# A 32-expert mixture stage: which experts are fetched early, the order of its matmuls, and its tables in fp32r

## The chip, the cores and the metric

One Trainium2 chip, one of its cores. The metric is the device time of one execution in microseconds; less is better. The kernel works on one sequence of 512 tokens with 1024 features, all in float32 ("fp32r" is the 32-bit type that TensorE takes in one pass where fp32 takes two; the kernel splits a number into an fp32r part and what is left of it where it needs both).

## The reference

Four layers run one after the other. The first two each have a mixer (three kinds of sequence mixing side by side) and then a mixture of experts. The last two are hybrid layers (two kinds of linear attention, then a layer norm). The change lies in the mixture, which in each of the first two layers computes:

```python
g_sel = top_1(x @ w_group + b_group)            # one of 4 groups for each token
e_local = top_2(expert logits of that group + bias)   # 2 of its 8 experts
weights = p_group * renormalised p_expert       # 2 weights for each token
# for every token and each of its two experts e:
h = silu(x @ w1[e]) * (x @ w3[e])               # 1024 -> 256
out[token] += weight * (h @ w2[e])              # 256 -> 1024
```

So 1024 pairs of a token and an expert are spread over 32 experts, unevenly. An expert's three matrices are 1 MB each, 96 MB for one layer, which don't fit on the core: they are streamed from HBM once for each layer.

## The kernel before

**Slots and groups.** The program is fixed, the routing isn't. `_slots` (L46) therefore lays out 12 groups of 128 slots. Each group is cut into strips of 32, and a position p (0 to 31) owns one, two or three strips of one group: 3 positions with 96 slots (B), 10 with 64 (M), 19 with 32 (S), in the order of `TURNS`. At run time experts are ranked by their token counts, and the expert of rank p takes position p. Tokens that don't fit go through a loop (`more`, L1363), which runs as often as windows of 64 are left over; with these inputs that is zero times, but the test for it is in the program, before group 8 (`CHECK`).

**Early experts.** Routing is done token tile by token tile (4 tiles of 128) beside the last matmuls of the mixer. After two tiles, `router_first` (L1133) takes the three experts with most tokens so far, gives them ranks 0, 1 and 2 for good, and starts to fetch them: 0 and 1 into the pool `wa`, 2 (started after a later chunk, L545) into the pool of width one, `hp`. Positions 0 and 1 are B and 2 is M. The order of the other 29 is known only after the fourth tile. Groups 0 to 3 hold the positions (2, 13, 14), (0, 15), (4, 16, 17), (1, 18).

**Streaming.** Five experts are resident at once: two in `wa`, two in `wp`, one in `hp`. `load` (L1201) gives each new expert the buffer of the resident one whose group is over first. All loads go through SyncE's queue, which is in order: first the new expert's w1 and w3, then the w2 that the expert before it is still owed. Each waits until the matmuls that read the evicted matrix are done. After the first two layers' mixture, the first weights of the next layer go the same way (`stage`), and are split into two fp32r parts by ScalarE and VectorE (`load_first`, pinned in the order of the program).

**The work of a group g** (main loop at the end of `moe_layer`, L1410 on):
- `one_hot`: for the next two groups, a 512 x 256 matrix that says which token sits in which slot (VectorE); once for every two groups.
- `gather`: brings the tokens into slot order, 8 blocks of 8 matmuls (L1237, L1238), an eviction each; once for every two groups, at odd g for g+1 and g+2.
- `up`: 128 matmuls on 32-column strips (L1310), then tanh on ScalarE (L1313) and two VectorE instructions (L1314, L1316).
- `table`: 4 matmuls of fp32, each in two passes (L1292), that give each slot its token and weight; then small VectorE work.
- `turned`: 2 transposes (L1323), evicted by ScalarE (L1325). `down`: 32 matmuls (L1341), evicted as two fp32r parts (L1343, L1344).
- `combine`: adds the group's results to the 512 tokens, 8 steps of 2 matmuls (L1354) and a VectorE add (L1355).

**What sets the order.** The loop is written as up, tables, gather and combine of the group before in turns, turned, down. But a planner reorders each engine's instructions at build time by its own idea of when each is ready; an engine then runs its list in order. Only an instruction passed to `keep_in_program_order` stays behind the one that was written before it on its engine. In the experts' stage before the change no matmul is pinned.

Of the kernel before, what the change touches and what calls it, by code (L numbers as in the profile page):

```python
# [9 lines left out]
F32 = mybir.dt.float32  # L10
# [35 lines left out]
def _slots():  # L46


    turns = TURNS.replace(" ", "")
    kinds = sorted(turns)  # L50
    kinds = kinds[0:2] + ["M"] + kinds[2:turns.count("B")] + kinds[turns.count("B") + 1:]
    size = [dict(B=BIG, M=MID, S=SMALL)[k] for k in kinds]
    free = {k: [p for p in range(len(kinds)) if kinds[p] == k] for k in "BMS"}
    assert len(size) == NE and sum(size) % 128 == 0
# [12 lines left out]
    return [base[p] for p in range(NE)], groups  # L67


BASE, GROUPS = _slots()  # L70
# [14 lines left out]
class Kernel:  # L85
# [42 lines left out]
    def constants(self):  # L128
# [21 lines left out]
        with self.tc.tile_pool(name="ctmp", bufs=1) as tp:  # L150
# [15 lines left out]
            for p in range(NE):  # L166
                b, c = BASE[p]
                nc.gpsimd.memset(self.tab[:, 0, p:p + 1], float(b))
                nc.gpsimd.memset(self.tab[:, 1, p:p + 1], float(c))
# [298 lines left out]
    def mix_layer(self, l, x, xp, xd):  # L468
        nc, a, tc = self.nc, self.a, self.tc
        with ExitStack() as st:  # L470
# [57 lines left out]
            for c, ts in ((0, (0, 1)), (1, (0, 1)), (2, (0, 1)), (3, (0,)), (3, (1,)),  # L528
# [15 lines left out]
                if (c, t) == (1, 3):  # L544
                    W[2] = self.expert_weights(l, third())  # L545
# [587 lines left out]
    def router_first(self, l, rp, wa, R):  # L1133
# [3 lines left out]
        cnt, scr = R["pc"][0], R["scr"]  # L1137
        m8 = rp.tile([128, 8], F32, name="fm8")
        i8 = rp.tile([128, 8], U32, name="fi8")
        V.max(m8, cnt)  # L1140
        V.max_index(i8, m8, cnt)
        fi = rp.tile([128, 3], F32, name="ffi")
        V.tensor_copy(fi, i8[:, 0:3])
        first = rp.tile([1, 3], I32, name="first")
        V.tensor_copy(first, fi[0:1])
        key = R["key"] = rp.tile([128, NE], F32, name="key")
        for i in range(3):
            V.tensor_scalar(scr, self.iota[:, 0:NE], fi[:, i:i + 1], 65536.0 * (3 - i), op0=OP.is_equal, op1=OP.mult)
# [32 lines left out]
    def moe_layer(self, l, x, wa, wp, W, R, hT, nxt=None):  # L1181
        nc, a, tc = self.nc, self.a, self.tc
        V = nc.vector
        with ExitStack() as st:
# [6 lines left out]
            held = {wa: [0, 1], wp: [], None: [2]}  # L1191
# [36 lines left out]
            def gather(oh, n, tag="st"):  # L1228

                m = 4 if tag == "st" else KT  # L1230
                for k in range(KT):
# [3 lines left out]
                    for t in range(NT):  # L1235
                        ts = slice(t * 128, (t + 1) * 128)
                        nc.tensor.matmul(p, hh[:, k, ts], oh[:, t], start=(t == 0), stop=False)  # L1237
# [36 lines left out]
            tv = mp.tile([128, NT, 4], F32, name="tv")  # L1274
            V.tensor_copy(tv[:, :, 0:1], self.tokv)
# [10 lines left out]
            V.tensor_copy(tv[:, :, 2:4], pw.rearrange("p i t -> p t i"))  # L1286

            def table(oh, base, s0, m):

                p = self.mx([m, 4])  # L1290
                for t in range(NT):
                    nc.tensor.matmul(p, oh[:, t, s0:s0 + m].bitcast(F32), tv[:, t], start=(t == 0), stop=(t == NT - 1))  # L1292
                f = mp.tile([m, 4], F32, name="tf", tag="tf", bufs=3)
                V.tensor_copy(f, p)
# [828 lines left out]
```

## Time and profile before

| | us |
|---|---|
| median of 3 runs (1758.17 to 1760.28) | 1758.62 |
| the profiled execution | 1759.24 |
| its span, first to last instruction | 1757.2 |
| experts' stage, layer 0: first gather to the last `down` | 266.4 |
| experts' stage, layer 1 | 265.3 |

The profiled execution is 0.6 us over the median. The profile's page gives busy time by engine (PE is TensorE's matmuls, PEld its weight loads, DVE VectorE, ACT ScalarE, SP SyncE), and in 40 slices the granted TensorE clock (1.00 is full speed) and the share of the transfer engines in use. The views behind it are the stretches of time with busy time of each engine, the waits (who waited for whom), and the instructions in order of time, where a bracket gives the idle time before an instruction and what ended it. A row of the last kind may merge instructions of one line that follow each other; its time then runs from the start of the first to the end of the last, and the next row can start before that end, since matmuls are pipelined.

### The profile page before, as it was taken

The numbers are of one execution on the slowest core, as the hardware profiler recorded it, in microseconds if no ns is written. First come the engines' busy times: TensorE is split into PE (matmuls) and PEld (weight loads), VectorE is DVE, ScalarE is ACT, GpSimd is POOL, SyncE is SP. The second block draws the span as 40 slices with busy tenths as digits, with TensorE's granted clock in tenths as the row PEclk, the third lists the DMA queues.
The fourth block names the chain that finished last, engine by engine and source line by source line (L and its number), as shares of the span: only waits on it lengthen the run. The fifth ranks groups of instructions, "written<-read, shape, count | busy, mean of one in ns | idle before, by whom it ended". The sixth has DMA issues, their size and how long they took to land. (4 is left out here: it accounts for less than half of the span.)

```text
span 1757.2 us, 38728 instructions
## 1 busy us (share of the span) xinstructions
PE 1640.4 (93%) x15762; PEld 1329.8 (76%) x15762; DVE 1069.5 (61%) x2777; ACT 679.7 (39%) x1807; POOL 126.4 (7%) x236
## 2 busy tenths in 40 slices
PE   7999997999999899998799999999999999999998
PEld 7779987665554777998766556487789898778988
DVE  6866755455444586676545545456767565676756
ACT  5656563111111565656311111145443424554340
POOL 1011011000000001102100000000000200000010
PEclk9999998999999999999799999999999999999999
DMA  5112315799897311231679989633311324231132
GB/s 161 44 44 82 112 49 241 286 421 392 315 419 268 119 45 44 82 113 49 258 292 419 374 331 418 259 122 81 88 52 51 122 73 129 74 88 51 51 121 72
DMA packets 132542, 299.22 MB, mean 170 GB/s; under 512 B 34160, under 2 KB 100670, under 8 KB 107784
## 3 DMA queue, kind: packets, MB, share of 16 engines
q1 hardware_dynamic: 129384, 287.46, 44.8%
q10 hardware_dynamic: 1760, 6.30, 0.9%
q0 software_dynamic: 1216, 2.93, 0.7%
q8 instruction: 126, 2.06, 0.5%
q14 instruction: 56, 0.46, 0.1%
HBM read 284.87 MB, written 9.44 MB: 167 GB/s over the span
## 5 line engine op out<-in xcount | busy, mean ns | idle before, releaser
L327 PE MATMUL acc<-w_hi,hT_hi 128*128 128x256 f32 (+2 forms) x1248 | 358.3, 287 | 3.6 <-ACT hT_hi L252 1.6
L328 PE MATMUL acc<-w_lo,hT_hi 128*128 128x256 f32 (+2 forms) x1248 | 356.9, 286 | 1.5 <-DVE w_lo L308 1.4
L329 PE MATMUL acc<-w_hi,hT_lo 128*128 128x256 f32 (+2 forms) x1248 | 353.5, 283 | 3.0 <-issue 1.7
L327 PEld LDWEIGHTS acc<-w_hi,hT_hi 128*128 128x128 f32 x1248 | 237.3, 190 | 8.0 <-ACT hT_hi L252 2.0
L329 PEld LDWEIGHTS acc<-w_hi,hT_lo 128*128 128x128 f32 x1248 | 237.8, 191 | 4.3 <-issue 1.9
L328 PEld LDWEIGHTS acc<-w_lo,hT_hi 128*128 128x128 f32 x1248 | 237.4, 190 | 3.8 <-DVE w_lo L308 2.3
L1310 PE MATMUL acc<-w,xt 128*32 128x256 f32 x3072 | 191.0, 389 | 5.9 <-DVEq L1366 5.9
L1310 PEld LDWEIGHTS acc<-w,xt 128*32 128x32 f32 x3072 | 104.3, 112 | 87.2 <-issue 25.7
L328 PE MATMUL acc<-hT_lo,w_hi 128*128 128x512 f32 x352 | 143.4, 407 | 0.0
L329 PE MATMUL acc<-hT_hi,w_lo 128*128 128x512 f32 x352 | 142.4, 405 | 0.0
L327 PE MATMUL acc<-hT_hi,w_hi 128*128 128x512 f32 x352 | 142.0, 403 | 0.0
L1237 PE MATMUL acc<-oh,hT_hi 128*128 128x256 f32 x384 | 100.4, 297 | 7.1 <-DVE oh L1225 3.4
L1341 PE MATMUL mx<-w,gT 128*32 128x512 f32 x768 | 92.1, 622 | 8.7 <-ACT gT L1325 8.6
L308 DVE TENSOR_TENSOR w_lo<-st,w_hi 128x1024 fp32r<-128x1024 f32 (+2 forms) x71 | 87.4, 1240 | 19.8 <-ACT w_hi L307 19.7
L1313 ACT ACTIVATE th<-acc 128x256 f32<-128x256 f32 x24 | 9.2, 385 | 227.6 <-PE acc L1310 227.6
L1238 PE MATMUL acc<-oh,hT_lo 128*128 128x256 f32 x384 | 96.6, 287 | 0.0
L307 ACT ACTIVATE w_hi<-st 128x1024 fp32r<-128x1024 f32 (+1 forms) x71 | 74.8, 1073 | 49.2 <-PE acc L329 28.6
L1344 DVE SCALAR_TENSOR_TENSOR yb<-mx,ws,yb 128x512 fp32r<-128x512 f32 x48 | 35.9, 748 | 93.3 <-ACT yb L1343 93.3
L1237 PEld LDWEIGHTS acc<-oh,hT_hi 128*128 128x128 f32 x384 | 75.7, 197 | 21.2 <-issue 8.5
L327 PEld LDWEIGHTS acc<-hT_hi,w_hi 128*128 128x128 f32 x352 | 68.1, 193 | 14.4
L1238 PEld LDWEIGHTS acc<-oh,hT_lo 128*128 128x128 f32 x384 | 75.9, 198 | 2.0
L328 PEld LDWEIGHTS acc<-hT_lo,w_hi 128*128 128x128 f32 x352 | 67.1, 191 | 13.6 <-issue 0.3
(607 smaller groups left out, 3195.8 us busy)
## 6 DMA issues: line engine op xcount, KB each, us to landing
w<-in_w_dram SPq DMA_DIRECT2D x192, 1024.0 KB
st<-in_w_in_dram SPq DMA_DIRECT2D x66, 512.0 KB
st<-in_w_out_dram SPq DMA_DIRECT2D x32, 512.0 KB
st<-in_w_in_dram SPq DMA_DIRECT2D x22, 520.0 KB
xd<-x ACTq DMA_DIRECT2D x12, 512.0 KB
x<-xd SPq DMA_DIRECT2D x12, 512.0 KB
x<-in_x_dram SPq DMA_DIRECT2D x8, 512.0 KB
out_dram<-x SPq DMA_DIRECT2D x8, 256.0 KB
```

The source lines that it names most:

```text
L307: q = [nc.scalar.activation(hi[:, sl], w, AF.Copy), nc.vector.tensor_tensor(lo[:, sl], w, hi[:, sl].bitcast(F32), op=OP.subtract)]
L308: nc.vector.tensor_tensor(lo[:, sl], w, hi[:, sl].bitcast(F32), op=OP.subtract)]
L327: self.nc.tensor.matmul(out, lh(k), rh(k), start=(k == ks[0]), stop=False)
L328: self.nc.tensor.matmul(out, lh(k), rl(k), start=False, stop=False)
L329: self.nc.tensor.matmul(out, ll(k), rh(k), start=False, stop=(k == ks[-1]))
L1237: nc.tensor.matmul(p, hh[:, k, ts], oh[:, t], start=(t == 0), stop=False)
L1238: nc.tensor.matmul(p, hl[:, k, ts], oh[:, t], start=False, stop=(t == NT - 1))
L1310: nc.tensor.matmul(ph[c:c + n, i], xt[k][:, s0 + c:s0 + c + n], w[i][:, k], start=(k == 0), stop=(k == KT - 1))
L1313: nc.scalar.activation(th, ph[:, 0], AF.Tanh, scale=0.5)
L1341: nc.tensor.matmul(py[c:c + n], gT[:, k, c:c + n], w[2][:, k, sl], start=(k == 0), stop=(k == 1))
L1344: V.scalar_tensor_tensor(yb[:, 1, sl], py, ws, yb[:, 0, sl].bitcast(F32), op0=OP.mult, op1=OP.subtract)
```

## The change

Three parts.

**Which experts come first.** Position 0 is now M and the B positions are 1 to 3. `router_first` ranks by count (ties by number), and takes the expert of rank 3 after two tiles for position 0, and the two with the fewest tokens for positions 30 and 31. The first group is now made of exactly these three, (0, 30, 31), then (1, 13), (4, 14, 15), (2, 16). Number and size of the early loads stay.

**The order of matmuls.** The first matmul of each block of the experts' stage (gather, up, both transposes, down, combine, table) is pinned; of `up` only the first one for w1, not the first one for w3. The loop is rewritten: after `up`, six steps of the combine of the group before (at odd g in turns with seven blocks of the gather), then `turned`, then the rest, then `down`. At group 7, before the test for left-over windows, the gather goes in turns with the combine of group 7 itself, which stood alone behind the loads of group 8 before. In the last group the next layer's first weights are loaded and split ahead of `up`, not behind `down`.

**Tables.** The four columns of token, slot and weights are kept as an fp32r part and a remainder, 8 columns, so that a table takes 4 one-pass matmuls; a small sum over the two parts replaces the copy.

```diff
 def _slots():
...
-    kinds = kinds[0:2] + ["M"] + kinds[2:turns.count("B")] + kinds[turns.count("B") + 1:]
+    kinds.remove(turns[0])
+    kinds.insert(0, turns[0])
...
+    free["S"] = free["S"][-2:] + free["S"][:-2]
...
+FIRST = (0, NE - 2, NE - 1)
+RANK = 3
...
     def router_first(self, l, rp, wa, R):
...
-        V.max(m8, cnt)
-        V.max_index(i8, m8, cnt)
+        V.scalar_tensor_tensor(key, cnt, float(NE), self.keyc, op0=OP.mult, op1=OP.add)
+        V.tensor_scalar(scr, key, -1.0, None, op0=OP.mult)
+        for i, k in enumerate((key, scr)):
+            V.max(m8[:, i], k)
+            V.max_index(i8[:, i], m8[:, i], k)
...
-        return {i: self.expert_weights(l, e(i), wa) for i in range(2)}, lambda: e(2)
+        return {FIRST[i]: self.expert_weights(l, e(i), wa) for i in range(2)}, lambda: e(2)
...
+                        if t == 0:
+                            tc.keep_in_program_order(q)
...
             tv = mp.tile([128, NT, 4], F32, name="tv")
+            tv2 = mp.tile([128, NT, 8], F32R, name="tv2")
...
+                V.tensor_copy(tv2[:, :, 0:4], tv)
+                V.tensor_tensor(tv2[:, :, 4:8], tv, tv2[:, :, 0:4].bitcast(F32), op=OP.subtract)
...
-                p = self.mx([m, 4])
+                p = self.mx([m, 8])
...
-                V.tensor_copy(f, p)
+                V.reduce_sum(f, p.rearrange("p (i n) -> p n i", i=2), axis=AX.X)
...
             for g in range(n):
                 loads(GROUPS[g])
                 if g == CHECK:
-                    run(combine(*last))
-                    last = None
                     more()
-                ahead = g % 2 and g + 1 < n
+                if g == n - 1:
+                    later()
+                    if nxt:
+                        self.staged = self.stage(nxt[0][0], wp)
+                        self.load_first(*nxt[0])
+                ahead, check = g % 2 and g + 1 < n, g + 1 == CHECK
...
-                sums = combine(*last) if last else None
-                if ahead:
-                    xt_next = []
-                    for step in gather(oh, 256):
-                        xt_next.append(step)
+                sums, rows, xt_next = combine(*last) if last else None, gather(oh, 256) if ahead else None, []
+                for i in range(8 if rows and not check else 6):
+                    if not check:
+                        run(rows, 1 if i < 7 else 0, xt_next)
+                    if i < 6:
                         run(sums, 1)
+                gT = turned(gg, 128)
+                if not check:
+                    run(rows, None, xt_next)
                 run(sums)
-                gT = turned(gg, 128)
                 last = down(gT, segs, 128, *tabs.pop(0))
+                if check:
+                    sums, last = combine(*last), None
+                    for i in range(8):
+                        run(rows, i % 2, xt_next)
+                        run(sums, 1)
+                    run(rows, None, xt_next)
                 if ahead:
                     xt, tabs = xt_next, tables(oh, g + 1)
-                if g == n - 1:
-                    later()
-                    if nxt:
-                        self.staged = self.stage(nxt[0][0], wp)
-                        self.load_first(*nxt[0])
             run(combine(*last, nxt and nxt[1]))
```

## Rows read from the trace of the kernel before

**Rows 1.** The page: busy time of each engine, share of the span, instructions.

```profile
PE 1640.4 (93%) x15762; PEld 1329.8 (76%) x15762; DVE 1069.5 (61%) x2777; ACT 679.7 (39%) x1807; POOL 126.4 (7%) x236
```

**Rows 2.** Stretches: the experts' stages of layers 0 and 1; from PEclk on: clock, transfers.

```profile
304.96:571.40 266.44, 248.23 (x2600) 155.81 (x2600) 130.12 (x311) 37.55 (x76) 0.00 (x0) 0.96 0.87 350
874.19:1139.50 265.31, 247.49 (x2600) 156.12 (x2600) 130.04 (x311) 37.41 (x73) 0.00 (x0) 0.97 0.88 353
```

**Rows 3.** Waits of TensorE, 304.9 to 582: total us, times, longest.

```profile
PE mx L1323 <- DVE gg L1316: 8.5, 7, 1.7
PE mx L270 <- DVE nss L446: 5.6, 1, 5.6
PE mx L1341 <- ACT gT L1325: 4.3, 8, 0.6
```

**Rows 4.** TensorE in order of time, start of the stage: start, us, line, count.

```profile
304.96 0.58 PE L1237 MATMUL acc<-oh,hT_hi 128*128 128x256 f32 x1 [1.33 <-DVE oh L1225]
...
316.17 1.95 PE L1292 MATMUL mx<-tv,oh 128*128 128x4 f32 x16
...
322.47 8.24 PE L1310 MATMUL acc<-w,xt 128*32 128x256 f32 x122
...
333.24 3.64 PE L1341 MATMUL mx<-w,gT 128*32 128x512 f32 x32 [0.47 <-ACT gT L1325]
```

**Rows 5.** TensorE in order of time, the last group.

```profile
556.86 7.10 PE L1310 MATMUL acc<-w,xt 128*32 128x256 f32 x124
565.62 0.41 PE L1323 MATMUL mx<-ident,gg 128*128 128x128 f32 x2 [1.66 <-DVE gg L1316]
566.56 5.34 PE L1341 MATMUL mx<-w,gT 128*32 128x512 f32 x32 [0.53 <-ACT gT L1325]
```

**Rows 6.** TensorE in order of time, one odd group in the middle.

```profile
384.40 0.73 PE L1354 MATMUL acc<-yb,to 128*128 128x512 f32 x2
...
394.67 0.38 PE L1323 MATMUL mx<-ident,gg 128*128 128x128 f32 x2
...
395.58 3.64 PE L1341 MATMUL mx<-w,gT 128*32 128x512 f32 x32
399.15 1.95 PE L1292 MATMUL mx<-tv,oh 128*128 128x4 f32 x16
400.96 0.94 PE L1354 MATMUL acc<-yb,to 128*128 128x512 f32 x3
...
404.99 7.09 PE L1310 MATMUL acc<-w,xt 128*32 128x256 f32 x122
```

**Rows 7.** All engines in order of time, behind the test for left-over windows.

```profile
496.08 8.91 PE L1310 MATMUL acc<-w,xt 128*32 128x256 f32 x132 [2.93 <-DVEq L1366]
```

**Rows 8.** Stretches of layer 0; the last two columns: transfer share, GB/s.

```profile
320.00:327.50 7.50, 6.73 (x78) 3.72 (x82) 2.86 (x9) 0.00 (x0) 0.00 (x0) 0.77 0.02 5
340.00:400.00 60.00, 58.95 (x622) 39.19 (x614) 32.11 (x68) 10.23 (x20) 0.00 (x0) 1.00 1.01 417
...
305.00:555.00 250.00, 233.99 (x2435) 149.12 (x2436) 123.66 (x299) 35.07 (x69) 0.00 (x0) 0.97 0.90 363
```

**Rows 9.** Waits of SyncE's transfer queue, 303 to 560: total, times, longest.

```profile
SPq L1177 <- PE acc L1310: 81.5, 18, 18.5
...
SPq L1177 <- PEq L1366: 5.5, 1, 5.5
```

**Rows 10.** SyncE in order of time, the next layer's first weights.

```profile
552.95 1.18 SPq L287 DMA_DIRECT2D st<-in_w_in_dram  x1
```

**Rows 11.** ScalarE and VectorE in order of time, end of layers 0 and 1's experts.

```profile
572.55 3.29 ACT L311 ACTIVATE w_hi<-st,again 128x256 fp32r<-128x256 f32 x8
...
573.88 3.25 DVE L312 SCALAR_TENSOR_TENSOR w_lo<-st,again,w_hi 128x256 fp32r<-128x256 f32 x8
...
1142.83 2.31 DVE L308 TENSOR_TENSOR w_lo<-st,w_hi 128x2080 fp32r<-128x2080 f32 x1
```

**Rows 12.** VectorE in order of time, `router_first` of layer 0.

```profile
264.80 0.20 DVE L1140 MAX8 fm<-mx 128x8 f32<-128x32 f32 x1 [0.86 <-PE mx L1119]
```

More of the change, by code (lines that the diff above doesn't have):

```diff
@@ L66, in _slots @@
             b, c = b + m, c - m
-    return [base[p] for p in range(NE)], groups
-BASE, GROUPS = _slots()
+    return [base[p][0] for p in range(NE)], size, groups
+BASE, SIZE, GROUPS = _slots()
+FIRST = (0, NE - 2, NE - 1)
+RANK = 3
 ALPHA = (2.0 * 2) ** 0.25
@@ L1188, in moe_layer @@
             rp = R["pool"]
-            held = {wa: [0, 1], wp: [], None: [2]}
+            held = {wa: list(FIRST[0:2]), wp: [], None: [FIRST[2]]}
             ends = {p: g for g, segs in enumerate(GROUPS) for _, _, p in segs}
@@ L1236, in gather @@
                         ts = slice(t * 128, (t + 1) * 128)
-                        nc.tensor.matmul(p, hh[:, k, ts], oh[:, t], start=(t == 0), stop=False)
+                        q = nc.tensor.matmul(p, hh[:, k, ts], oh[:, t], start=(t == 0), stop=False)
+                        if t == 0:
+                            tc.keep_in_program_order(q)
                         nc.tensor.matmul(p, hl[:, k, ts], oh[:, t], start=False, stop=(t == NT - 1))
@@ L1286, in moe_layer @@
             V.tensor_copy(tv[:, :, 2:4], pw.rearrange("p i t -> p t i"))
+            pack()
             def table(oh, base, s0, m):
-                p = self.mx([m, 4])
+                p = self.mx([m, 8])
                 for t in range(NT):
-                    nc.tensor.matmul(p, oh[:, t, s0:s0 + m].bitcast(F32), tv[:, t], start=(t == 0), stop=(t == NT - 1))
+                    o, w = oh[:, t, s0:s0 + m], tv2[:, t]
+                    q = nc.tensor.matmul(p, *((o, w) if m == 128 else (o.bitcast(F32), w.bitcast(F32))), start=(t == 0),
+                                         stop=(t == NT - 1))
+                    if t == 0 and m == 128:
+                        tc.keep_in_program_order(q)
                 f = mp.tile([m, 4], F32, name="tf", tag="tf", bufs=3)
-                V.tensor_copy(f, p)
+                V.reduce_sum(f, p.rearrange("p (i n) -> p n i", i=2), axis=AX.X)
                 c = mp.tile([m, 2], F32, name="tc", tag="tc", bufs=2)
@@ L1309, in up @@
                         for c, n, w in segs:
-                            nc.tensor.matmul(ph[c:c + n, i], xt[k][:, s0 + c:s0 + c + n], w[i][:, k],
-                                             start=(k == 0), stop=(k == KT - 1))
+                            q = nc.tensor.matmul(ph[c:c + n, i], xt[k][:, s0 + c:s0 + c + n], w[i][:, k],
+                                                 start=(k == 0), stop=(k == KT - 1))
+                            if i == k == 0 and m == 128:
+                                tc.keep_in_program_order(q)
                 th = mp.tile([m, DE], F32, name="th", tag="th", bufs=1)
@@ L1322, in turned @@
                 for k in range(2):
[L1323 removed]
+                    q = nc.tensor.transpose(pT[:, k], g[:, k], self.ident[0:m, 0:m])
+                    if m == 128:
+                        tc.keep_in_program_order(q)
                 gT = mp.tile([128, 2, m], F32, name="gT", tag="gT", bufs=1)
@@ L1340, in down @@
                         for c, n, w in segs:
-                            nc.tensor.matmul(py[c:c + n], gT[:, k, c:c + n], w[2][:, k, sl],
-                                             start=(k == 0), stop=(k == 1))
+                            q = nc.tensor.matmul(py[c:c + n], gT[:, k, c:c + n], w[2][:, k, sl],
+                                                 start=(k == 0), stop=(k == 1))
+                            if k == 0 and m == 128:
+                                tc.keep_in_program_order(q)
                     nc.scalar.activation(yb[:, 0, sl], py, AF.Copy, scale=ws)
@@ L1353, in combine @@
                         for i in range(2):
-                            nc.tensor.matmul(p, to[:, t * 128:(t + 1) * 128], yb[:, i, sl], start=(i == 0), stop=(i == 1))
+                            q = nc.tensor.matmul(p, to[:, t * 128:(t + 1) * 128], yb[:, i, sl], start=(i == 0), stop=(i == 1))
+                            if i == 0 and not rows and to.shape[0] == 128:
+                                tc.keep_in_program_order(q)
                         V.tensor_tensor(x[:, t, sl], p, x[:, t, sl], op=OP.add)
```

24 lines of the change are left out of this document (13 added, 11 removed).

## The prediction

> **What bounds the kernel now.** I read the page first: TensorE is busy 93% of the span and no other engine above 61% [rows 1]. The change touches only the experts' stage of two layers, 266.4 and 265.3 us long; there TensorE is busy 248 and 247 us and the transfer engines 0.87 and 0.88 of the time at 350 GB/s [rows 2]. So two things are nearly full in this stage, and both need a count.
>
> TensorE first. The pieces at full clock: an `up` 7.05 us (128 matmuls, 7.09 for 122 with the tail), a `down` 3.57 (395.58 to 399.15), a pair of tables 1.81 (399.15 to 400.96), a combine that stands alone 4.03 (400.96 to 404.99), seven gather blocks in turns with eight combine steps 10.27 (384.40 to 394.67), so about 0.9 a gather block and 0.46 a combine step; a pair of transposes 0.35 [rows 6]. Without waits the stage is 10.7 for the first gather, 5 x 7.3 more of gather, 12 x 7.05 of up, 12 x 3.57 of down, 6 x 1.81 of tables, 11 x 8 x 0.46 of combine, 12 x 0.35 of transposes: 230 us. The stage takes 266, so some 36 us go elsewhere. The waits show the larger part of the causes: the transposes wait 8.5 us in seven groups for the gated product gg, the `down` that follows 4.3 us in eight groups for ScalarE's copy [rows 3], and 2.9 us go at the test for left-over windows [rows 7]. The pattern is in the last group: combine has already run ahead of `up`, nothing is left to do while gg is made, 1.66 and then 0.53 us are idle, and the `down` behind these gaps takes 5.34 instead of 3.6 us [rows 5]. The `up` behind the test takes 8.91 [rows 7], and one at the start 8.24 [rows 4], in a stretch in which the granted clock is 0.77 on the mean, part of it at the lower level [rows 8]. The rest are fragments of `up` and of the gather that the planner put between other blocks.
>
> Transfers second. Where they are never short of work they move 417 GB/s, so 1 MB takes 2.5 us [rows 8]. 29 experts of three loads are 87 loads, 217 us, of the 250 us between 305 and 555; the share of 0.90 says the same [rows 8]. SyncE's queue waits 81.5 us for `up` to let go of a buffer [rows 9]: transfers wait for TensorE, not the other way round. No wait of TensorE for a weight shows.
>
> **The change part by part.** *The order.* I rebuild layer 0 from these pieces in the new order. First gather 10.65 as before (the clock is low there and nothing of it changes). Group 0: up 7.05, two tables 0.9, then gg is late by what is left of 2.1 (the steps on ScalarE and VectorE between an `up` and its transposes: 563.96 to 565.62 is idle, and the end of `up` overlaps them [rows 5]), so 1.2, transposes 0.4, 0.5 for the copy, down 3.55: 13.6. An odd group with a gather (1, 3, 5, 9): 7.05 + 11.2 (8 blocks and 8 steps) + 0.4 + 3.55 + 0.9 of tables: 23.1. An even group (2, 4, 6, 10) and the last: 7.05 + 4.03 + 0.4 + 3.55 and 0.2 of a wait: 15.2; six combine steps (2.8 us) cover gg's 2.1, two (0.9) the copy's 0.9. Group 7 has a combine more: 27.1. Group 8 has none left: 3.0 for the test, 7.05 + 0.5 of low clock, 2.1 + 0.4 + 0.5 + 3.55: 17.1. Sum 10.65 + 13.6 + 4 x 23.1 + 27.1 + 17.1 + 5 x 15.2 = 236.9, that is 29.5 under layer 0 and 28.4 under layer 1 [rows 2].
>
> *Tables* are in this sum: 16 matmuls for two tables take 1.95 with the tail [rows 4]; eight one-pass matmuls at the gather's spacing (0.9 / 8 = 0.113) take 0.9. Below, a matmul of 8 columns might cost nothing (another 11 us over both layers); above, as much as now (11 us lost). I take the gather's, which loads the same 128x128 fp32r weights. The two packing instructions and the sum are a few VectorE instructions of about 0.2 us [rows 12], on an engine busy half the stage [rows 2].
>
> *Early experts.* Nothing of group 0 is on its way any more when the order is known. Loads of 1 and 13 (five of 1 MB) run from about 304.6 to 317; the next waits for `up` of group 0, about 319 and 322.6, where now the transfers stand still from 320 to 327.5 [rows 8]. From there 82 loads are 205 us; with some 5 us more at the test, where SyncE stops too (5.5 us now [rows 9]), the last one lands at about 533. TensorE wants the last w1 at 527 and the last w3 at 530 by the sum above, and these come 7 and 5 us ahead of the last load, at 526 to 530. So transfers are level with TensorE only at the end. I charge 3 us a layer, bounds 0 and 10. By counting the reference's routing on its inputs, the expert taken for position 0 ends with 58 and 49 tokens, under 64, and the two rarest stay under 17, so no window is left over in either layout. `router_first` gains five small VectorE instructions of about 0.2 us [rows 12] ahead of the first loads; those loads have until 315 to land, so this is hidden; without that cover it is 1 us a layer, and I put 0.4 a layer.
>
> *Next layer's weights.* They now split before the last `up`, not behind `down`: 3.29 us of ScalarE and 3.25 of VectorE leave the way of the rows of the next layer, for which TensorE waits 5.6 us at the end of layer 0 [rows 3, 11]. The second add of the last combine stands 3.3 us behind that block, so I take 3.3 there and, for the 2.31 us instruction of layer 1, 1.0, since TensorE has other work there [rows 11]. But their load is queued behind the last w2, which waits for `down` of group 10, as the load at 552.95 does now [rows 10]; it lands 7 us later, as the last `up` ends. If the planner lists the split ahead of the last tanh, gg is late by 3 us of landing and 3.3 of splitting, if behind, by nothing. I take 3 a layer, bounds 0 and 6.4.
>
> Sum: layer 0 -29.5 + 3 + 3 = -23.5, layer 1 -28.4 + 6 = -22.4, the ends -3.3 and -1.0, the router 0.8. That is -49.4 from the profiled 1759.2, or 1709.8; the median lies 0.6 lower, so I say 1710.
>
> **The rivals.** *A, loads set the pace.* If transfers stand still for the tenth of the time that they do now [rows 8], 25 us and not the 9 of my count, the last load ends at 304.6 + 217.5 + 25 = 547, and the last w3 at 542.5, so `down` ends at about 553: the stage is 248 long, 18.5 and 17 shorter, less 3 each; with the ends 1759 - 33 = 1726. For it speaks that buffers are let go later when combine stands between `up` and `down`; against it that the buffers that groups 2 to 6 need are let go two groups earlier. *B, the order is only half there.* Only first matmuls are pinned, and VectorE's list isn't. If two adds of 0.6 us (the spacing in a combine) stand ahead of gg in each group, 1.2 x 12 a layer comes back, 29 us: 1738. *C, slower.* The mean of 350 GB/s [rows 2] is a pace and not the result of waiting: each load then takes 3.0, 87 of them 261, the last ends at 304.6 + 261 + 9 = 575, `down` at 579, 7.6 behind now, and 3 for the split, in both layers: 1759 + 21 - 4 = 1776. It decides from 2.9 us a load on (87 x 2.9 = 252 leaves the layer 2 us longer with the split, which the ends give back). Against it stand 60 us on end at 417 GB/s [rows 8]. The Trainium skill, "DMA: Bandwidth & Descriptors", section "Where 436 GB/s comes from", says that from HBM about 358 GB/s is the limit of a core, which would be near case C and leave no gain (an estimate from the page: 2.93 us a load); these rows disagree with it, and the measurement decides. *D, no change*, if B and the table's upper bound come together with a late split: 49 - 29 - 11 - 7, within 3 us.
>
> **How the numbers follow.** My sum, within its bounds, 0.74; A 0.09; B 0.08; C 0.05; D 0.04. The best end is both charges at 0 and half of the tables' lower bound: 1710 - 12 - 6 = 1692. The high end takes in A and B and rests at the sum with all charges at their upper bound: 10 - 3 and 6.4 - 3.0 twice, and two thirds of the VectorE delays of B, 1710 + 21 + 11 = 1742. Left out are C, D and some of the case of the tables at nothing. About 0.2% is what a measurement of this kernel can tell from no change: faster by that is my sum, A and B, 0.91; the same 0.04; slower 0.05.
>
> **What would show it.** Right: both stages near 240 us; waits of the transposes for gg under 3 us a layer instead of 8.5; tables at half their time; no fragments of `up`; transfers at 417 GB/s for most of the stage. Wrong: `up` stretched over 8 us or idle ahead of it behind late loads (A, C); waits for gg as long as now (B); a ScalarE that splits weights between the last `up` and its tanh (the charge of 3); the same table time. The prediction falls most easily by transfers, which are level with TensorE in it and have no cover left.

## The result and the profile after

The changed kernel takes 1708.03 us (median; 1706.28 to 1708.35) beside 1758.39 us (1752.86 to 1760.28) of the kernel before on the same chip: ratio 0.9717, 95% interval 0.9694 to 0.9739. The forecast was 1710 us. When the pair was timed again with later experiments, the times were 1713.70 (1708.99 to 1718.94) and 1755.57, ratio 0.9755 (0.9725 to 0.9785). So medians of one and the same kernel differ by up to 6 us between two timings, which decides how much a small difference below may mean.

The profiled execution took 1706.28 us. A stage is counted here, in both kernels, from the first matmul of its first gather to the end of its last `down` (layer 0 from 304.96 to 571.90 before, from 300.47 to 543.61 after):

| stretch | before | after | difference | forecast |
|---|---|---|---|---|
| up to the stage of layer 0 | 304.96 | 300.47 | -4.5 | +0.4 |
| stage of layer 0 | 266.94 | 243.14 | -23.8 | -23.5 |
| between the stages | 302.29 | 299.64 | -2.7 | -2.9 |
| stage of layer 1 | 265.39 | 242.98 | -22.4 | -22.4 |
| behind | 617.62 | 617.97 | +0.4 | -1.0 |

The page's engine line, beside [rows 1], and the two stages as stretches, beside [rows 2] (columns: stretch, length, busy us of TensorE, its weight loads, VectorE, ScalarE and GpSimd, granted clock, share of the transfer engines, GB/s):

```profile
PE 1600.9 (94%) x15666; PEld 1308.7 (77%) x15666; DVE 1070.6 (63%) x2793; ACT 680.1 (40%) x1807; POOL 125.9 (7%) x236
...
300.47:543.61 243.14, 232.68 (x2552) 149.90 (x2552) 128.13 (x316) 40.11 (x82) 0.00 (x0) 0.96 0.95 384
843.25:1086.23 242.98, 232.72 (x2552) 149.80 (x2552) 128.12 (x310) 40.10 (x75) 0.00 (x0) 0.96 0.96 385
```

The stage is 23 us shorter; 15 of them are TensorE's own work (248 to 233 us busy), the rest are waits. Two groups of matmuls make up most of the 15: in layer 0 the tables fall from 11.7 to 6.2 us busy, and `up` by some 8 us a layer. The page's line of `up`, both layers, before and then after (count, busy us, mean ns):

```profile
L1310 PE MATMUL acc<-w,xt 128*32 128x256 f32 x3072 | 191.0, 389 | 5.9 <-DVEq L1366 5.9
```

```profile
L1333 PE MATMUL acc<-w,xt 128*32 128x256 f32 x3072 | 174.5, 386 | 10.1 <-PEq L1397 10.1
```

As many matmuls of the same mean length fill 16.5 us less, so more of them overlap: they now run in whole blocks of 128, where the planner had cut them into fragments. What is left of the waits, for TensorE in layer 0 from 300 to 580 us (columns: line waited for, us in total, times, longest):

```profile
PE acc L1333 <- PEq L1397: 5.1, 1, 5.1
PE mx L274 <- DVE nss L450: 3.4, 2, 2.6
PE acc L1246 <- DVE oh L1234: 2.0, 4, 1.3
PE acc L1383 <- DVE to L1361: 2.0, 1, 2.0
PE mx L1348 <- DVE gg L1341: 1.6, 1, 1.6
...
PE mx L1348 <- DVE tc L1322: 1.2, 1, 1.2
PE mx L1368 <- ACT gT L1352: 1.0, 2, 0.5
```

Against [rows 3]: the transposes' wait for gg went from 8.5 us in seven groups to 1.6 in one (group 8, behind the test), the `down`'s wait for gT from 4.3 to 1.0. New is the first line, to which the experiments come back. The first gather waits for its one-hot table about as long as before (2.0 us; 2.1 before), now in four pieces. One even group shows the written order (TensorE's timeline: start, us, line, tile, count):

```profile
389.83 7.11 PE L1333 MATMUL acc<-w,xt 128*32 128x256 f32 x128
396.88 0.74 PE L1383 MATMUL acc<-yb,to 128*128 128x512 f32 x2
...
399.33 0.63 PE L1383 MATMUL mx<-yb,to 128*128 128x512 f32 x2
399.80 0.38 PE L1348 MATMUL mx<-ident,gg 128*128 128x128 f32 x2
399.93 0.71 PE L1383 MATMUL acc<-yb,to 128*128 128x512 f32 x2
400.48 0.63 PE L1383 MATMUL mx<-yb,to 128*128 128x512 f32 x2
401.04 3.64 PE L1368 MATMUL mx<-w,gT 128*32 128x512 f32 x32
404.49 1.69 PE L1333 MATMUL acc<-w,xt 128*32 128x256 f32 x28
```

Twelve matmuls of combine (six steps of two) stand between `up` and the transposes, four between these and `down`; nothing waits, and a group takes 14.66 us.

### The profile page after: what moved, and what is told of

Same layout as the page of the kernel before. It is cut to its first block, busy times and chain, and to the rows that moved or that the text cites. A ratio compares the mean times of both kernels' runs of the same rounds, so it can differ in the third digit from the quotient of the medians.

```text
span 1704.2 us, 38593 instructions
## 1 busy us (share of the span) xinstructions
PE 1600.9 (94%) x15666; PEld 1308.7 (77%) x15666; DVE 1070.6 (63%) x2793; ACT 680.1 (40%) x1807; POOL 125.9 (7%) x236
## 3 DMA queue, kind: packets, MB, share of 16 engines
q8 instruction: 126, 2.06, 0.5%
## 5 line engine op out<-in xcount | busy, mean ns | idle before, releaser
L1333 PE MATMUL acc<-w,xt 128*32 128x256 f32 x3072 | 174.5, 386 | 10.1 <-PEq L1397 10.1
L1333 PEld LDWEIGHTS acc<-w,xt 128*32 128x32 f32 x3072 | 100.2, 112 | 82.1 <-issue 20.6
L311 ACT ACTIVATE w_hi<-st 128x1024 fp32r<-128x1024 f32 (+2 forms) x71 | 74.6, 1073 | 48.4 <-PE acc L333 28.5
L1386 DVE TENSOR_TENSOR x<-mx,x 128x512 f32<-128x512 f32 x96 | 65.7, 684 | 22.4 <-PE mx L1383 22.4
L1339 DVE SCALAR_TENSOR_TENSOR th<-th,acc 128x256 f32<-128x256 f32 x24 | 10.1, 421 | 110.3 <-ACT th L1338 110.3
```

The costliest lines, as they stand in the source:

```text
L311: q = [nc.scalar.activation(hi[:, sl], w, AF.Copy), nc.vector.tensor_tensor(lo[:, sl], w, hi[:, sl].bitcast(F32), op=OP.subtract)]
L1333: q = nc.tensor.matmul(ph[c:c + n, i], xt[k][:, s0 + c:s0 + c + n], w[i][:, k], start=(k == 0), stop=(k == KT - 1))
L1339: V.scalar_tensor_tensor(th, th, 1.0, ph[:, 0], op0=OP.add, op1=OP.mult)
L1386: V.tensor_tensor(x[:, t, sl], p, x[:, t, sl], op=OP.add)
```

## The experiments

Each was made from the changed kernel, except the early experts alone. The first four were timed together, with the kernel before at 1757.23 us, then the next four (1756.09), then the last four (1755.57). Ratios are to the kernel before of the same timing.

**Without the early experts.** `FIRST` is (0, 1, 2) again, with the old slots and the old `router_first`.

```diff
-FIRST = (0, NE - 2, NE - 1)
+FIRST = (0, 1, 2)
```

> The kernel after, with the early experts and the layout of the slots as they were before (ranks 0, 1, 2 early; group 0 needs two experts that are fetched only when the order is known). Order of matmuls, tables and the early split stay. Theory: with the fixed order TensorE wants the second small expert of group 0 earlier than it can land, and transfers start two experts behind, so the stage grows by 4 to 8 us a layer: 1716 to 1724, against 1708. Rival 1: transfers have cover all the same and the early experts are worth nothing: 1708. Rival 2: the 4.5 us that layer 0 gained ahead of its experts' stage belong to the new choice of early experts (its extra VectorE work moves a wait of TensorE, and with it the stretch of low clock): then the low clock near 256 to 263 and 287 to 293 us is back in the profile here and the start of the first gather is near 305 instead of 300.5.

1709.15 us (1706.19 to 1709.80), ratio 0.9716 (0.9686 to 0.9746): the changed kernel's own. The theory fell, the first rival holds: once the order is fixed this part is worth nothing that can be measured. Its stage of layer 0 is even shorter (240.56 us) and what lies ahead of it as long as before (305.15): the second rival holds too, and the section on the prediction comes back to it.

**Tables in fp32 again**

```diff
-                p = self.mx([m, 8])
+                p = self.mx([m, 4])
...
+                    q = nc.tensor.matmul(p, oh[:, t, s0:s0 + m].bitcast(F32), tv[:, t], start=(t == 0), stop=(t == NT - 1))
```

> The kernel after, with the tables as 4 fp32 matmuls of 4 columns as before. Theory: a pair of tables takes 1.81 us again instead of 0.98 and nothing runs beside it on TensorE, so 12 pairs over both layers cost 10 us: 1718. Rival: they are hidden behind loads or VectorE, 1708 to 1710.

1723.38 us (1720.98 to 1729.64), 0.9814 (0.9780 to 0.9849): 15 us more. A pair of tables has its old price, where the changed kernel shows 1.05 us for 8 (the first line is this kernel's, the second the changed one's):

```profile
353.66 1.95 PE L1309 MATMUL mx<-tv,oh 128*128 128x4 f32 x16
```

```profile
350.62 1.05 PE L1312 MATMUL mx<-tv,oh 128*128 128x8 f32 x8
```

Six pairs of 0.9 are 5.4 us a layer; its stages are 3.4 and 5.3 us longer, although the wait at the test is 2.0 and 1.8 us here instead of 5.1 and 4.9, since TensorE's branch takes 2.0 and 0.35 us and 6.1 in the changed kernel. This led to the last four runs. The other 6 us of the 15 lie outside the stages. Within them, an odd group with its two tables takes 24.32 us against 23.60 at the same clock (1.00), which is 0.7 a pair. Group 8 of layer 0, behind the test, takes 17.52 us at a granted clock of 0.75 against 15.17 at 0.86, which uses up most of what the shorter wait saved.

**No fixed order in the stage**

```diff
-                            if i == k == 0 and m == 128:
-                                tc.keep_in_program_order(q)
```

(and the same at the gather, the tables, the transposes, `down` and combine)

> The kernel after, with no matmul of the experts' stage pinned; the loop is written as in the kernel after. Theory: the planner lets combine run ahead of up again, the waits of the transposes for gg come back (8.5 us a layer against 2.9 now) with the fragments of up: 15 us a layer, 1738. Rival: the way the loop is written does it and the pins add nothing: 1704 to 1710, the lower end if the pinned first gather, which takes 12.5 us now and took 10.7 before, is quicker without pins.

1733.41 us (1731.06 to 1737.18), 0.9859 (0.9826 to 0.9893): 25 us more, near the theory's 1738. Both stages take 257 us, the wait for gg is back where it was in [rows 3], and `up` is in fragments again:

```profile
PE mx L1342 <- DVE gg L1335: 8.5, 6, 1.7
```

```profile
L1329 PE MATMUL acc<-w,xt 128*32 128x256 f32 x3072 | 188.4, 389 | 10.0 <-PEq L1385 10.0
```

**Next layer's weights behind the last `down` again**

```diff
-                if g == n - 1:
-                    later()
-                    if nxt:
-                        self.staged = self.stage(nxt[0][0], wp)
-                        self.load_first(*nxt[0])
...
+                if g == n - 1:
+                    later()
...
```

(the five lines stand at the end of the loop's body)

> The kernel after, with load and split of the next layer's first weights behind the last down again. Theory: the move is worth little, since in the kernel after the split stands between the last transposes and the last results on ScalarE and VectorE and TensorE waits 2.0 us for the token matrix behind it and 2.6 for the first rows of the next layer: 1708 to 1711. Rival, as predicted blind: the move took 3.3 us off the end of layer 0 and 1 off that of layer 1: 1712.5.

1714.53 us (1707.11 to 1715.81), 0.9739 (0.9702 to 0.9776). The long wait of [rows 3] at the end of layer 0 is back:

```profile
PE mx L274 <- DVE nss L450: 6.0, 2, 5.6
```

It stands in the place of 2.0 and 2.6 us above, so the part is worth about 1 us there. The 6.5 us between the medians are about what one kernel shows in two timings; more than 1 us is not shown. In its profile 3.8 us more stand in the stage of layer 1, in groups 0 and 8 at a lower clock (0.80 and 0.74 against 0.89 and 0.86), which the edit doesn't touch.

**The old loop with the pins**

```diff
-                for i in range(8 if rows and not check else 6):
...
-                gT = turned(gg, 128)
-                if not check:
-                    run(rows, None, xt_next)
                 run(sums)
+                gT = turned(gg, 128)
                 last = down(gT, segs, 128, *tabs.pop(0))
```

> The loop over the groups is written as before (all eight combine steps ahead of the transposes, gather in turns with it from its sixth step on as before, the combine of the last group ahead of the test, next layer's weights behind the last down), everything else as in the changed kernel, the pinned first matmuls too. Theory (the written order matters as much as the pins): nothing stands between the transposes and the down, so ScalarE's copy of gT (about 0.9 us) is open in each group but where the planner finds work; 24 groups x some 0.5 us more than now are 10 us, the late split of the next layer's weights 4 more: 1718 to 1724, waits for gT near 5 us a layer, stages near 248 us. Rival 1 (pins alone carry it): 1708 to 1714, stages at 243 to 245. Rival 2 (with pins and the old text the gather cannot run while gg is made, since it is pinned behind the combine): waits for gg come back to 5 us and more a layer as well, 1730 or more.

1732.14 us (1730.26 to 1735.94), 0.9856 (0.9812 to 0.9900): 24 us more. Now all eight steps of combine stand ahead of the transposes, and every group has the gap behind them that the theory named:

```profile
402.03 0.62 PE L1383 MATMUL mx<-yb,to 128*128 128x512 f32 x2
402.49 0.38 PE L1348 MATMUL mx<-ident,gg 128*128 128x128 f32 x2
403.40 3.19 PE L1368 MATMUL mx<-w,gT 128*32 128x512 f32 x25 [0.53 <-ACT gT L1352]
...
PE mx L1368 <- ACT gT L1352: 6.3, 12, 0.5
```

The stages are 248.8 and 247.3 us, 5.7 and 4.3 more than after, as the theory said, and with the late split 2.5 us come in between them. That is half of the 24: 12.9 us more lie behind the stage of layer 1, in work that the edit doesn't touch; there TensorE shows a lower clock in more stretches. I can't say why. So about 12 us are shown for the edit, 10 for the written order in the stages and 2.5 for the late split. The time is that of the second rival (1730 or more), but not by its mechanism: the wait for gg is 1.7 us, in one group.

**The first gather left free**

```diff
-                        if t == 0:
+                        if t == 0 and pin:
...
+            xt, tabs, last = list(gather(oh, 256, pin=False)), None, None
```

> Only the first gather of each layer is left without fixed first matmuls; the others keep them. Theory: pinned, it waits for every quarter of the one-hot table and took 12.5 us against 10.65 us before the change, so this gives back about 1.8 us a layer: 3.6 us less than the changed kernel, near 1704.5, first gather near 10.7 us. Rival: the gather was long because TensorE stands at the lower clock there, whatever the order, and the planner fills the gaps with the same blocks: no difference within 1 us.

1710.66 us (1708.39 to 1716.55), 0.9735 (0.9700 to 0.9769): no faster as a whole. In the stages the theory holds and more: the first gather runs from 301.87 to 312.41, 10.5 us against 12.5, and the stages are 239.9 and 239.4 us, 3.2 and 3.6 less, at a mean granted clock of 0.97 and 0.98 instead of 0.96. The profiled execution loses as much behind the stage of layer 1 (625.3 us against 618.0); why is open.

**Next layer's weights ahead of the last w2**

```diff
                 if g == n - 1:
-                    later()
                     if nxt:
                         self.staged = self.stage(nxt[0][0], wp)
+                    later()
+                    if nxt:
```

> In the last group the next layer's weights are loaded ahead of the last w2 instead of behind it. Theory: they land some 3 us earlier, before the last up ends, so ScalarE's and VectorE's 3.3 us of splitting stand ahead of gT instead of ahead of the last scaled rows; TensorE's wait at the end of layer 0 (2.00 for the onehot, 2.64 for the row sums) shrinks by 2 to 3 us, and the last w2 is 1.5 us later, which nothing waits for: 1 to 2 us less than the changed kernel in all, stage and end of layer 0 together. Rival (the charge of 3 us a layer in the prediction): the split now stands ahead of gg or of its tanh, the transposes of the last group wait 3 us longer, and the sum is 1 to 3 us more than the changed kernel.

1712.00 us (1710.35 to 1712.84), 0.9736 (0.9704 to 0.9769): no gain. The rival is right on the mechanism: a second wait of the transposes for gg, of 2.3 us, appears in layer 0, its stage grows by 1.7 us, and what lies between the stages shrinks by 0.8.

**The early experts alone**, from the kernel before

```diff
+    kinds.remove(turns[0])
+    kinds.insert(0, turns[0])
...
+FIRST = (0, NE - 2, NE - 1)
```

> The kernel before with only the part on the early experts: the three experts fetched early are those of the first group, with the slots that go with them; no fixed order, tables in fp32, loop as before. Theory (this part is worth nothing, since TensorE never waits for a weight in either form): within 3 us of before, 1755 to 1761; transfers no longer stand still at the start of the stage, which changes no time. Rival 1 (it is worth what was read at the start of the stage, where transfers stood still from 320 to 327 us): 5 to 10 us a layer less, 1740 to 1748. Rival 2 (in the unplanned order the weights of the middle groups come later than now, and the up fragments grow): 3 to 8 us more, 1761 to 1767. Also looked at: the granted clock in the 40 us ahead of the stage of layer 0, where the change showed the higher level; if it goes with this part, it shows the higher level here, and the stage starts near 301 instead of 305 us.

1749.93 us (1743.87 to 1759.06), 0.9957 (0.9933 to 0.9980): 6 us less, between the theory and its first rival. The stages are 262.8 and 260.7 us, 4.1 and 4.7 less than before; the wait for gg is 6.8 us in five groups. So in the planner's order the part has a worth, alone about 6 us; on top of the fixed order it shows none.

**The changed kernel again, 88 idle matmuls, and a shorter jump.** The kernel with the fp32 tables had put the question. TensorE's branch at the test (its line in the kernel before, then after; columns: count, ns least, median and most, first and last start):

```profile
L1366 PEldq COMPARE_BRANCH  x2: 347/396/445, 492.1 to 1061.0; - x2
```

```profile
L1397 PEldq COMPARE_BRANCH  x2: 6105/6106/6108, 469.0 to 1011.5; - x2
```

And the transfer queues while it lasts in the changed kernel, 469.0 to 475.1 us (queue, packets, MB, share of 16 engines):

```profile
q1 hardware_dynamic: 333, 2.40, 95.7%
q8 instruction: 1, 0.02, 1.1%
q14 instruction: 2, 0.02, 0.8%
```

One block of instructions is read by q8 during it, in layer 1 too (1011.5 to 1017.6, without the two small packets of q14); over the whole span 126 such blocks hold 2.06 MB, 16 KB each. The read starts at 472.5, 3.5 us into the branch, and takes 1.1 us. In the 0.5 us of the branch at 492.1 in the kernel before none is read. The Trainium skill, "Runtime: NRT & Kernel Launch", section "Instruction fetch mechanics", says that instructions come in blocks of 16 KiB and that a taken branch to a block outside the engine's current window waits for it to be read; these rows agree. If so, where the program stands in its blocks decides, and this depends on every instruction ahead of it.

> The changed kernel itself, for comparison with the three that follow on the same chip: 1706 to 1712 us, TensorE's branch at the test 6.1 us in both layers, one 16 KB block of instructions read during it.

```diff
             nc.tensor.matmul(pm, own[0:NE, 3:4], self.ones[0:NE, 0:1], start=True, stop=True)
+            pd = self.mx([128, 128])
+            for _ in range(48 if l else 40):
+                nc.tensor.matmul(pd, self.ident_bf, self.ident_bf, start=True, stop=True)
```

> The changed kernel with 40 (layer 0) and 48 (layer 1) bf16 matmuls of 128x128 that nothing reads, put among the small matmuls of routing, so that TensorE's program is at the test as long as it was with the tables in fp32 (which had 40 and 88 matmuls more up to there). Theory (the branch at the test is long because the block of instructions that it jumps to is not on the chip yet, and this hangs on where in its 16 KB blocks the program stands): the branch takes 0.3 to 2.0 us as with the fp32 tables, no block is read during it, the wait of 5.1 us for TensorE's branch goes and one of 2.9 us for VectorE's, as before the change, stays: 2.2 us a layer less. The added matmuls (some 0.06 us each, 2.5 us) lie in the routing, where TensorE waits 6.5 us in pieces, and cost 0 to 2.5 us a layer. Together 1703 to 1709. Rival 1 (the branch is long because the new order lets TensorE come to it earlier, while the transfers are full): still 6 us, 1708 to 1713. Beside it: work in the waits of routing may raise the granted clock at 295 to 305 us; if so the first gather shrinks from 12.5 to 11 us.

```diff
-                    with tc.For_i(0, many, 1) as j:
-                        e = nc.sync.value_load(who[:, bass.ds(j, 1)], min_val=0, max_val=NE - 1)
...
```

> The changed kernel without the loop over left-over windows inside the test (its body is not run on these inputs; what is left out is the treatment of tokens beyond an expert's slots). Theory (a jump over less code lands in a block that is on the chip already): branch under 1 us, TensorE's wait at the test 2.9 us or less instead of 5.1: 4 to 5 us less than the changed kernel, 1702 to 1706. Rival (it hangs on where the blocks begin and not on the length of the jump): either 6 us again, or short by chance in one layer. SyncE's wait at the test and the order around it stay.

The changed kernel gave 1713.70 us. With the 88 added matmuls that nothing reads: 1700.72 us (1697.38 to 1705.57), 0.9670 (0.9634 to 0.9706), which lies wholly below the changed kernel's 0.9725 to 0.9785. With the shorter jump: 1706.12 us (1704.25 to 1717.57), 0.9729 (0.9687 to 0.9771), which overlaps the changed kernel's interval. Their branches:

```profile
L1400 PEldq COMPARE_BRANCH  x2: 347/736/1125, 465.4 to 1007.6; - x2
```

```profile
L1397 PEldq COMPARE_BRANCH  x2: 213/224/236, 473.5 to 1012.6; - x2
```

So with the added matmuls the theory stands: TensorE comes to the test even earlier (465.4 us, layer 0), the transfer engines are as full as ever (98% for q1), and the branch takes 1.1 and 0.35 us; what the edit changed ahead of it is the length of the program. Where it took 1.1 to 2.0 us (layer 0 of this kernel, of the last one below and of the one with fp32 tables), the read of a block had begun 0.4 to 1.3 us ahead of it (464.1, 464.5 and 474.8 us), and each of these branches ends some 2.5 us after the read's start, as the long ones do: the same wait, it seems, begun earlier. In the six other kernels that add no matmul ahead of the test and keep the loop behind it, the branch takes 5.9 to 6.2 us, whatever their order. What remains of TensorE's wait is 2.4 and 1.8 us for VectorE's branch.

The shorter jump shows less than it was made for. The branch is short (0.2 us, although a read began 0.5 us ahead of it, at 473.0), but the order around the test did not stay: on TensorE the branch now stands inside the `up` of group 8, behind 82 of its 128 matmuls:

```profile
470.45 4.94 PE L1333 MATMUL acc<-w,xt 128*32 128x256 f32 x82
475.54 2.79 PE L1333 MATMUL acc<-w,xt 128*32 128x256 f32 x46
```

So these matmuls cover the wait for TensorE's branch and for VectorE's alike, and groups 7 and 8 take 41.4 us in both layers instead of 47.9 and 47.7. What the length of the jump does by itself is not shown. The stages are 4.9 and 6.2 us shorter than the changed kernel's in this timing (243.5 and 242.8). From 475 to 480 us the clock is 1.00 (2.4 GHz) here, while the changed kernel, idle for most of 470 to 475, shows 0.55 there; 1.3 and 1.6 us are given back to a wait that the loads come to, below.

The added matmuls do a second thing. The same stretch of the changed kernel, and then of this one:

```profile
295.00:300.00 5.00, 0.90 (x10) 0.58 (x9) 4.30 (x29) 1.21 (x2) 1.31 (x2) 0.50 0.07 11
300.00:305.00 5.00, 3.83 (x12) 2.95 (x13) 4.84 (x23) 0.52 (x2) 0.00 (x0) 0.50 0.95 383
305.00:310.00 5.00, 5.00 (x29) 5.00 (x29) 1.94 (x10) 0.95 (x2) 0.00 (x0) 0.62 1.00 418
```

```profile
295.00:300.00 5.00, 1.62 (x18) 1.37 (x18) 4.29 (x28) 1.34 (x2) 1.44 (x2) 0.50 0.06 10
300.00:305.00 5.00, 5.00 (x52) 4.90 (x50) 4.97 (x25) 0.53 (x2) 0.00 (x0) 0.78 0.93 364
305.00:310.00 5.00, 5.00 (x45) 5.00 (x44) 2.46 (x11) 1.42 (x3) 0.00 (x0) 1.00 1.00 421
```

In layer 0 they run from 299.22 to 303.05, beginning at the lower clock (0.50, that is 1.2 GHz), in a time in which TensorE would wait for the one-hot table; the gather then begins 2.4 us later, at 302.86, but takes 7.9 us instead of 12.5 because the clock is at its full level for most of it. Net, the first `up` starts at 310.73 instead of 312.94. In layer 1 the 48 matmuls put the gather off by 3.3 us, and it takes 7.7 us instead of 12.5.

In the two profiles of this timing (1705.57 us with the added matmuls, 1713.15 without) the stages are 9.3 and 7.5 us shorter. Most of that stands at their start, where the clock is at its full level earlier: 4.8 and 4.7 us in the first gather, 1.4 and 1.3 in group 0; groups 7 and 8, with the test between them, are 3.1 and 1.5 shorter. But between the stages it takes 308.37 us instead of 299.91. Of these 8.5 us 3.3 are the 48 matmuls; for the rest the granted clock is lower in the routing of layer 1 (0.55 from 824 to 829 us), and whether the added matmuls bring that about is open. So the 13 us between the medians are measured, but only in part explained.

**Both**, the free first gather and the added matmuls:

> The free first gather together with the added matmuls of the shift, as a candidate for a faster kernel. Theory: stages of 239.9 and 239.4 us, as with the free first gather alone, less 2.2 us each at the test: 237.5 each; against the changed kernel 5 us each in the stages, less what the added matmuls cost: 1700 to 1705. Rival (what the stage gains by the free first gather was clock time, and it turns up again in the attention behind it, as the 5.4 us more at the lower clock there showed): 1705 to 1710.

1699.93 us (1696.36 to 1711.94), 0.9693 (0.9656 to 0.9730). Stages of 234.4 and 234.6 us, as with the added matmuls alone (234.1 and 235.3): once TensorE is busy ahead of the gather, no cost of its order shows. The stages are shorter than the theory's 237.5, but between them it takes 307.66 us, as long as with the added matmuls alone. The two are the fastest kernels here, 13 us below the changed one, and can't be told from one another.

## Why the prediction was right, point by point

**The order** gave what was counted, and by the mechanism that was named: the waits for gg and gT fell, and `up` is no longer in fragments. Rival B did not come: the wait for gg is 1.6 us in one group. With pins or written order undone, the wait of the transposes for gg or of `down` for gT is back, and the stages are 14, or 4 to 6, us longer. The pieces of layer 0, each up to the next `up` (the pause at the test with group 8):

| piece | forecast | measured | difference |
|---|---|---|---|
| first gather | 10.65 | 12.47 | +1.8 |
| group 0 | 13.6 | 15.06 | +1.5 |
| odd groups, four | 23.1 | 23.59 | +2.0 |
| group 7 | 27.1 | 27.55 | +0.5 |
| group 8 with the test | 17.1 | 20.29 | +3.2 |
| five others | 15.2 | 14.68 | -2.6 |
| stage without charges | 236.9 | 243.1 | +6.2 |
| charges, loads and split | 6 | 0 | -6 |

So the mechanism was right, but that -23.5 was met so closely is luck: two errors cancel, 6 us of charges that did not come and 6 us of pieces that were put too short. Five terms were mis-sized, the odd groups by 0.5 us each and four more. "Nothing of it changes", of the first gather, was wrong: its first matmuls are pinned, so it stops three times more for the quarters of the one-hot table (0.7 us behind its start), and it stays at the lower clock until about 308.8 (0.62 on the mean from 305 to 310). Group 0 has the wait of 1.2 us that was forecast, for a table's result and not for gg, but its `down` takes 4.93 instead of 3.55 at a granted clock of 0.71. The test was put at 3.0 us as before, and took 5.1, for TensorE's own branch; the `up` behind it takes 9.11 us, where 7.55 was forecast, at the lower clock and not behind a late load. And an even group is shorter than the sum of its parts read from a mixed order: its two transposes take 0.13 us of it (399.80 to 399.93) instead of 0.4, `down` 3.45 instead of 3.55, and there is no wait of 0.2.

The range's upper end was added up wrongly: two thirds of B's 28.8 us are 19, not 11, which makes 1750 in place of 1742. The measured time is far from either.

**The loads** did not cost the 3 us charged, nor did any rival on them come true: from 340 to 400 us the transfers move 409 GB/s, and no `up` waits for a weight. But "level with TensorE only at the end" is shown by the kernel with the shorter jump, whose TensorE comes to the `up` of the last group at 522.64 instead of 528.80 and after six matmuls meets a late weight there, in layer 1 too (1.6 us):

```profile
524.54 7.09 PE L1333 MATMUL acc<-w,xt 128*32 128x256 f32 x122 [1.29 <-DMA w<-in_w_dram]
```

With the added matmuls TensorE is there at 522.19 and waits for nothing: its first `up` starts 2.5 us earlier (310.73 against 313.21), so it is ahead from the first group on; that its buffers therefore come free earlier is likely, but not shown.

**The split** of the next layer's weights was charged 3 us ahead of gg and credited 3.3 at the end; neither came. It is listed behind gT, where the prediction's cheap case had it (ScalarE's timeline in the last group of layer 0):

```profile
535.96 0.39 ACT L1338 ACTIVATE th<-acc 128x256 f32<-128x256 f32 x1 [6.19 <-PE acc L1333]
539.20 0.38 ACT L1352 ACTIVATE gT<-mx 128x256 f32<-128x256 f32 x1 [2.85 <-PE mx L1348]
539.48 3.29 ACT L315 ACTIVATE w_hi<-st,again 128x256 fp32r<-128x256 f32 x8
```

There it still stands ahead of the last adds and of the one-hot for the last combine on VectorE (its part of the split from 540.16, 3.24 us; the one-hot at 545.11), for which TensorE now waits 2.0 us. From the end of `down` to the first matmuls for the next layer's rows it is 7.94 us, where it was 8.24. So the 3.3 us credited at the end of layer 0 were the wrong term: the split still stands on that way. The 2.7 us that the stretch between the stages lost are thus hardly this; how much of it is the clock, in the profile of one execution, stays open.

**The tables** cost 0.98 us a pair by their spacing (350.62 to 351.60), 0.9 forecast, so six pairs save 5.0 us a layer where 5.4 were counted. In the kernel with fp32 tables the stages are 3.4 and 5.3 us longer, 6.5 and 8.4 if the 3.1 us that it gains at the test are added back; what is over 5.4 of that goes with a lower clock, in group 8 of both layers (17.5 and 17.6 us against 15.2) and in group 0 of layer 1 (17.5 against 15.1).

**Early experts** had no gain of their own in the sum, rightly. Their 0.4 us a layer in `router_first` can't be seen, since the stretch ahead became 4.5 us shorter. That was not forecast, and is at least in part TensorE's clock. Ten microseconds of the routing in the kernel before, after, and in the changed kernel with the old experts:

```profile
255.00:265.00 10.00, 9.56 (x55) 9.25 (x55) 3.42 (x19) 5.92 (x7) 4.59 (x5) 0.66 0.01 2
```

```profile
255.00:265.00 10.00, 8.69 (x75) 8.33 (x74) 6.03 (x33) 6.02 (x7) 4.68 (x5) 1.00 0.01 2
```

```profile
255.00:265.00 10.00, 9.78 (x59) 9.45 (x58) 3.50 (x19) 5.96 (x7) 4.60 (x5) 0.66 0.01 2
```

At 1.00 TensorE gets through 75 matmuls where it does 55 at 0.66. It goes with the early experts in all kernels here, the one with them alone among them (1.00); by which way was not settled. How much it is worth isn't settled either: with the new early experts the stage begins anywhere from 300.5 to 303.5 us, at 301.90 in the changed kernel profiled again and at 303.35 with the early experts alone, since another stretch at the lower clock, near 290, comes and goes. What the stage of layer 0 gained in the kernel with the old experts (240.56 us), in its first gather and in group 0, offset half of it.

## What to carry to other kernels

Where one engine is full and its gaps are the latencies of a short chain (matmul, activation, product, transpose), putting enough independent matmuls between the links and pinning their order is worth counting link by link: here six steps cover gg and two the copy. A sum by pieces must give each piece the clock and the waits of its new neighbours, above all the first piece behind a quiet stretch. And a small difference may be where the code happens to lie: move it before explaining it.

## What the runs showed of the hardware

TensorE's branch at the test takes 5.9 to 6.2 us in the runs in which a 16 KB block of instructions is read during it; the read itself starts 3.5 us into the branch and takes 1.1 us. Where a read began 0.4 to 1.3 us ahead of the branch and the branch waited for it, it takes 1.1 to 2.0 us, elsewhere 0.2 to 0.45. Whether the full data queue (96% of the transfer engines) lengthens this was not tested. Forty matmuls without use, put where TensorE waits in layer 0, put the gather off by 2.4 us and took it from 12.5 to 7.9 us, by the clock; 48 in layer 1 cost 3.3 us and took it from 12.5 to 7.7, but the stretch between the stages became 8.5 us longer.
